# Output projection and first gate chunk of a two-layer trunk: the last three K pairs one token tile after the other, in an order by hand

## The chip, the cores and the metric

The kernel runs on one core of a Trainium2 chip. The core has five engines with an instruction queue each: TensorE (PE in the profile; its weight loads are listed as PEld), VectorE (DVE), ScalarE (ACT), GpSimd (POOL) and SyncE (SP), which here only issues DMAs. The metric is the device time of one execution in microseconds (us). Before the change the median of three runs is 2180.88 us (2180.05 to 2183.07).

## The reference

A trunk of two layers works on 256 tokens of width 2048, in fp32:

```
for l in range(DEPTH):                       # 2 layers
    h = rms_norm(x, pre_mix_norm[l])
    m = hybrid_mixer(h, ...)                 # h @ w_in, two kinds of attention, mix @ w_o
    x = x + rms_norm(m, post_mix_norm[l])
    h = rms_norm(x, pre_ffn_norm[l])
    f = (silu(h @ w_gate[l]) * (h @ w_up[l])) @ w_down[l]      # 2048 -> 5632 -> 2048
    x = x + rms_norm(f, post_ffn_norm[l])

rms_norm(x, g) = x * rsqrt(mean(x * x) + 1e-6) * g
```

The change lies where `mix @ w_o` ends, its norm is added to `x`, and the product of the new `x` with `w_gate` and `w_up` begins.

## The kernel before, in words

**Tiles.** The 256 tokens are two token tiles, t = 0 and 1, of 128. A product accumulates over K = 2048, that is 16 K tiles of 128, taken in eight *pairs* `kp`. Output columns are taken in chunks of 512: four for the output projection (c = 0 to 3), eleven for gate and up together.

**Split operands.** Every fp32 operand is split in a rounded part and a rest. For weights ACT writes `hi` (L307) and DVE `lo = raw - hi` (L317), 128x1024 elements each, that is a pair's two K tiles by 512 columns. A product of two such operands is three matmuls of 128x128 by 128x512 (hi hi, lo hi, hi lo). A *unit* (L560) of one token tile is a pair by 512 columns: six matmuls.

**Sevens.** For some pairs two chunks and two token tiles are taken together in seven products instead of eight (`seven_products`): they use sums of token blocks (`pair_sums`, L1237, then `token_sums`, L1091 to L1102: `s`, rounded to `sh` on ACT, its rest `sl` on DVE) and mixed weights (`mixed_weights`). For the latter a pair of weight tiles is loaded as `G` and `T`; POOL adds a half of G's data into `T` by an accumulating DMA (L258); ACT rounds `hi` and `Th`, DVE works out `lo`, differences in `T` (L290), sums in `G` (L291) and the rests `Tl` (L281).

**Loads.** Weights come in tiles of 512 KB, all in one stream order. SP issues plain tiles `raw` (L241, four buffers), `G` (L230) and `T` (L257). A load into a `raw` buffer waits for DVE to have taken the rest of the tile four before it. There are six buffers for `hi` and six for `lo`.

**Order.** Most instructions are ordered by a scheduler that lays out each engine's queue at build time. Within `tc.manual_schedule(engines=...)` the named engines take the order of the program text. `tc.issue_after(x)` keeps an instruction behind x in its queue; `weights(i, ahead)` emits the roundings of the stream's tiles up to `ahead` tiles beyond i.

**The stage.** The output projection's chunks 2 and 3 take pairs `LATE_O` = 4, 5, 0, 1, 6, 2 with both token tiles at once (5 and 6 as sevens; after pair 6 the parts that the sevens share are worked out by `shared_part` and added). Then `LAST_O` = 3, 7 go token tile by token tile, in an order by hand for ACT and DVE (L1185 on): four units of t = 0, the evacuation (`evac_sum`: multiply by the gain, ACT's square for the norm), `rescale` for t = 0 (the norm's root by Ln, Exp and a Newton step, then x = x + r * mg for four quarters of 512 columns, L627), then four units of t = 1, and after each of them one quarter of t = 0's new x is turned: four transposes on PE into one PSUM bank (L485), four roundings with the gain on ACT (L488), four rests on DVE (L493), giving the stationary tiles `xF`. After the block, t = 1 is evacuated, rescaled and turned quarter by quarter at high priority. `inv_rms` squares x again (L512, eight ACT instructions of 128x512) for the feed-forward norm's factor `rs`, which is only used at the end of a chunk.

**The gate's first chunk.** It takes the pairs in the order 0, 1, 3, 2, 7, 4, 6, 5 (`FIRST_ORDER`). Pairs 0 and 1 go token tile by token tile (t = 0 with both, then t = 1 with both), then 3, 2, 7 with both, 4 and 6 as sevens (L1084 to L1086), and 5 last. The plain pairs are `eight` (L1250): 24 matmuls for two token tiles. PE's order is the scheduler's throughout. `FORM_AT` says ahead of which pair of which chunk the sums of a seven's pair are emitted: here pair 4's ahead of the second of the remaining pairs (n = 1), pair 6's ahead of the third (n = 2).

Both layers run the same stage: about 376 to 442 us in layer 0, 1462 to 1528 us in layer 1.

## Time and profile before

| | |
|---|---|
| median of the runs | 2180.88 us (2180.05 to 2183.07) |
| profiled execution | 2183.48 us, of which 2181.7 us span |
| mean granted TensorE clock | 0.999 |
| PE busy | 2166.0 us (99%), 9944 matmuls |
| DVE busy | 1920.7 us (88%) |
| ACT busy | 1400.4 us (64%) |
| POOL busy | 260.5 us (12%) |
| L317 rests on DVE | 468 of 1220 ns |
| L307 roundings on ACT | 490 of 1053 ns |

A profile has one row for an instruction, or for several alike that follow each other: start in us from the span's start, length, engine, line, operation, output <- inputs, shape, count, and in brackets the idle time before it with what ended it. A matmul's length overlaps with the next one's: what it costs is the distance between starts. In a windows row stand the stretch, its length, then for each engine its busy time and the number of its instructions, PEclk (the granted clock, 1.00 is full), the DMA engines' busy share and GB/s. In a row of waits stand what waited, for what, the sum in us, the number and the longest.

### The profile page before, as it was taken

To read this page: it belongs to the slowest core of one execution; us is meant where nothing else is said; L and a number is where in the kernel's file an instruction comes from. 1 tells how busy PE (TensorE), PEld (TensorE's weight loads), DVE (VectorE), ACT (ScalarE), POOL (GpSimd) and SP (SyncE) were. 2 spreads that over 40 slices of the span, in tenths; PEclk is the share of its full clock that TensorE was granted. 3 is DMA by queue.
4 is the path that set the end of the run, shared out by engine and by line. 5 is a ranking of instruction groups with operands and counts; after the bars stand their busy time and mean duration, and the time that the engine had idled before them with its cause. 6 is when DMAs were issued, how large, how long until landed. Compare 5 with 4: busy or idle time off the path is not lost.

```text
span 2181.7 us, 28784 instructions
## 1 busy us (share of the span) xinstructions
PE 2166.0 (99%) x9944; PEld 1781.7 (82%) x9944; DVE 1920.7 (88%) x2657; ACT 1400.4 (64%) x2089; POOL 260.5 (12%) x243
## 2 busy tenths in 40 slices
PE   9999999999999999999999999999999999999998
PEld 7888888788888888888878888887888888888886
DVE  7888658899999999999878886589999999999997
ACT  7666665756666656666665666657666666576664
POOL 1100000031222221000010000000212222200000
PEclk9999999999999999999999999999999999999999
DMA  9544555488887767767465555555888877768683
GB/s 323 194 164 174 193 184 176 165 300 234 239 258 229 226 231 233 239 223 258 149 241 174 172 174 188 191 164 191 286 237 241 262 222 227 240 225 244 204 268 100
DMA packets 140851, 471.49 MB, mean 216 GB/s; under 512 B 16016, under 2 KB 17040, under 8 KB 140192
## 3 DMA queue, kind: packets, MB, share of 16 engines
q1 hardware_dynamic: 121952, 436.03, 57.7%
q0 software_dynamic: 18176, 33.07, 9.2%
q8 instruction: 78, 1.28, 0.2%
q14 instruction: 69, 0.57, 0.1%
q10 hardware_dynamic: 576, 0.54, 0.1%
HBM read 461.19 MB, written 8.39 MB: 215 GB/s over the span
## 4 chain that ended last, share of the span: by engine, by line
PE 94%; DVE 3%; ACT 2%; issue 1%; DMA 0%; SPq 0%; DVEq 0%; ACTq 0%
PE c L1250 19%; PE in L1084 7%; PE in L1086 7%; PE in L1085 7%; PE dn L1357 4%; PE dn L1356 4%; PE dn L1359 4%; PE p L1085 3%; PE c L1084 3%; PE p L1084 3%; PE p L1086 3%; PE c L1085 3%; PE c L1086 3%; PE o L569 2%; PE o L571 2%; PE o L570 2%
## 5 line engine op out<-in xcount | busy, mean ns | idle before, releaser
L317 DVE TENSOR_TENSOR lo<-raw,hi 128x1024 fp32r<-128x1024 f32 x468 | 561.9, 1220 | 103.3 <-ACT hi L307 102.3
L307 ACT ACTIVATE hi<-raw 128x1024 fp32r<-128x1024 f32 x490 | 501.5, 1053 | 102.3 <-DMA raw<-in_weights_in_turn_dram 41.8
L1250 PE MATMUL c<-hi,xF 128*128 128x512 f32 x1280 | 345.9, 391 | 1.5 <-DVE xF L493 1.5
L1250 PEld LDWEIGHTS c<-hi,xF 128*128 128x128 f32 x1280 | 238.3, 188 | 50.3 <-DVE xF L493 2.0
L258 POOL DMA_DIRECT2D T<-in_weights_in_turn_dram x126 | 111.2, 883 | 1373.8 <-DMA T<-in_weights_in_turn_dram 716.6
L1250 PE MATMUL c<-lo,xF 128*128 128x512 f32 x640 | 198.2, 390 | 2.5 <-DVE lo L317 2.5
L279 ACT ACTIVATE Th<-G 128x1024 fp32r<-128x1024 f32 x126 | 133.1, 1056 | 79.8 <-DVE G L291 78.6
L281 DVE TENSOR_TENSOR Tl<-G,Th 128x1024 fp32r<-128x1024 f32 x126 | 153.9, 1221 | 10.1 <-ACT Th L279 10.1
L1356 PE MATMUL dn<-hi,jh 128*128 128x512 f32 x416 | 162.0, 389 | 0.0
L1357 PE MATMUL dn<-lo,jh 128*128 128x512 f32 x416 | 161.8, 389 | 0.0
L307 ACT ACTIVATE hi<-G 128x1024 fp32r<-128x1024 f32 x126 | 132.9, 1055 | 44.6 <-DMA G<-in_weights_in_turn_dram 27.8
L281 DVE TENSOR_TENSOR lo<-T,hi 128x1024 fp32r<-128x1024 f32 x126 | 159.6, 1266 | 0.3 <-ACT hi L279 0.2
L279 ACT ACTIVATE Th<-T 128x512 fp32r<-128x512 f32 x126 | 79.7, 633 | 118.6 <-DVE T L290 113.3
L291 DVE TENSOR_TENSOR G<-G,T 128x1024 f32<-128x1024 f32 x126 | 153.5, 1218 | 1.8
L1250 PEld LDWEIGHTS c<-lo,xF 128*128 128x128 f32 x640 | 120.1, 188 | 28.1 <-DVE lo L317 3.0
L317 DVE TENSOR_TENSOR lo<-G,hi 128x1024 fp32r<-128x1024 f32 x108 | 131.6, 1219 | 12.3 <-ACT hi L307 12.2
L279 ACT ACTIVATE hi<-T 128x1024 fp32r<-128x1024 f32 x126 | 132.2, 1049 | 12.1 <-PE c L1086 10.6
L1084 PE MATMUL in<-hi,xT 128*128 128x512 f32 x328 | 131.0, 401 | 0.6 <-DVE xT L862 0.6
L1084 PE MATMUL in<-hi,xI 128*128 128x512 f32 x328 | 131.1, 401 | 0.0
L1085 PE MATMUL in<-lo,xI 128*128 128x512 f32 x328 | 128.0, 390 | 0.3 <-DVE lo L317 0.3
L1085 PE MATMUL in<-lo,xT 128*128 128x512 f32 x328 | 127.8, 391 | 0.4 <-DVE lo L891 0.4
L1359 PE MATMUL dn<-hi,jl 128*128 128x512 f32 x416 | 128.0, 389 | 0.0
(485 smaller groups left out, 4954.2 us busy)
## 6 DMA issues: line engine op xcount, KB each, us to landing
raw<-in_weights_in_turn_dram SPq DMA_DIRECT2D x490, 512.0 KB, 4.6
T<-in_weights_in_turn_dram SPq DMA_DIRECT2D x126, 512.0 KB, 5.3
G<-in_weights_in_turn_dram SPq DMA_DIRECT2D x126, 512.0 KB, 5.4
T<-in_weights_in_turn_dram POOLq DMA_DIRECT2D x126, 256.0 KB, 6.1
GU<-in_weights_in_turn_dram SPq DMA_DIRECT2D x32, 512.0 KB, 6.5
V<-in_weights_in_turn_dram SPq DMA_DIRECT2D x8, 512.0 KB, 3.7
away_ffn<-x SPq DMA_DIRECT2D x8, 512.0 KB, 8.2
xd<-away_ffn SPq DMA_DIRECT2D x8, 512.0 KB, 9.4
```

What stands on the lines that cost most here:

```text
L279: nc.scalar.activation(h, w, AF.Copy)
L281: newest_rest[i] = nc.vector.tensor_tensor(out=l, in0=w, in1=h.bitcast(F32), op=ALU.subtract)
L291: nc.vector.tensor_tensor(out=g, in0=g, in1=t2.unsqueeze(1).to_broadcast([P, 2, CW]), op=ALU.add)
L307: nc.scalar.activation(hi, raw, AF.Copy)
L317: rest = nc.vector.tensor_tensor(out=lo, in0=raw, in1=hi.bitcast(F32), op=ALU.subtract)
L1084: nc.tensor.matmul(a, sh, hi, start=first, stop=False, skip_group_check=open_sums[0])
L1085: nc.tensor.matmul(a, sh, lo, start=False, stop=False, skip_group_check=open_sums[0])
L1086: return nc.tensor.matmul(a, sl, hi, start=False, stop=last, skip_group_check=open_sums[0])
L1250: nc.tensor.matmul(a, stat[part], w[j][:, kk, :], start=first and kk + n == 0, stop=last and kk == 1 and n == 2)
L1356: nc.tensor.matmul(accs[c, t], sh, hi[:, kk, :], start=first, stop=False, skip_group_check=open_sums[0])
L1357: nc.tensor.matmul(accs[c, t], sh, lo[:, kk, :], start=False, stop=False, skip_group_check=open_sums[0])
L1359: nc.tensor.matmul(accs[c, t], sl, hi[:, kk, :], start=False, stop=last, skip_group_check=open_sums[0])
```

## The change

- Pair 2, the last of `LATE_O`, joins `LAST_O`: all six units of t = 0 (pairs 2, 3, 7 by chunks 2 and 3), then all six of t = 1. The shared parts of the sevens are worked out between t = 0's units.
- PE joins ACT and DVE in the order by hand, which now reaches into the gate's first chunk: pairs 0 and 1 (`first`, `second`) of t = 0, then of t = 1.
- `rescale` is taken apart (`root_of`, a generator in three steps, and `rescaled`, one quarter), and so is `transposed` (`turned_x`, `rounded_x`, `rest_of_x`). Inside the order by hand only quarters 0 and 1 of x are rescaled and turned: quarter 0 of t = 0 between t = 1's units, the others between the units of the gate. Quarters 3 and 2 follow behind `newest`, the last rest of quarter 1.
- `rounded_next` puts the next weight tile's rounding on ACT at one place and its rest on DVE at a later one.
- `inv_rms` is emitted ahead of the gate's fifth pair (n = 2), its squares behind `newest`.
- Both pair sums, 4 and 6, are emitted ahead of the fifth pair.
- In the stream's load order that results, four `raw` tiles go ahead of the first two `T` and `G`.

The numbers of matmuls, roundings, rests and loads are the same. The core of the diff:

```diff
-FORM_AT = {(0, 1): 4, (0, 2): 6, (0, 5): 5, (1, 3): 2, (2, 4): 3}
+FORM_AT = {(0, 2): (4, 6), (0, 5): (5,), (1, 3): (2,), (2, 4): (3,)}
...
+    def rounded_next():
+        i = fed[0]
+        fetch(i + 1)
+        raw = raws[i]
+        hi = wpool.tile([P, 2, CW], F32R, tag="hi", bufs=6, name=f"hi{i}")
+        nc.scalar.activation(hi, raw, AF.Copy)
+        lo = wpool.tile([P, 2, CW], F32R, tag="lo", bufs=6, name=f"lo{i}")
...
+        def rest(eng=nc.vector):
+            r = eng.tensor_tensor(out=lo, in0=raw, in1=hi.bitcast(F32), op=ALU.subtract)
...
-    def inv_rms(t, pool, nm, parts=None):
+    def inv_rms(t, pool, nm, parts=None, behind=None):
...
+                with tc.issue_after(behind.ins) if behind else nullcontext():
+                    nc.scalar.activation(junk, x_part(t, h * CW, CW), AF.Square, accum_out=part[:, h : h + 1])
...
-        for kp in LATE_O:
+        for kp in LATE_O[:-1]:
...
-        last_o = [(c, kp) for c in (2, 3) for kp in LAST_O]
-        with tc.manual_schedule(engines={mybir.EngineType.Activation, mybir.EngineType.DVE}):
-            feed(idx + 6)
-            for n, (c, kp) in enumerate(last_o):
-                unit({0: accs[c, 0]}, mix, idx + n, kp, (0,), False, kp == LAST_O[-1], 0)
-                if kp == LAST_O[-1]:
-                    evac_sum(pool, accs[c, 0], mg, ssm, gpost, c, 0, f"o{l}")
-            rescale(mg, ssm, 0, f"o{l}")
-            for n, (c, kp) in enumerate(last_o):
...
-                unit({1: accs[c, 1]}, mix, idx + n, kp, (1,), False, kp == LAST_O[-1], 0)
-                transposed(0, 32 + l * KT, xT, cols=(n,))
...
-        with tc.high_priority(offset=URGENT):
-            evac_sum(pool, accs[3, 1], mg, ssm, gpost, 3, 1, f"o{l}", True)
-            rescale(mg, ssm, 1, f"o{l}", lambda t, c: transposed(t, 32 + l * KT, xT, cols=(c,)))
...
+        late = [(c, LATE_O[-1]) for c in (2, 3)] + [(c, kp) for c in (2, 3) for kp in LAST_O]
...
+        by_hand = {mybir.EngineType.Activation, mybir.EngineType.DVE, mybir.EngineType.PE}
+        with tc.manual_schedule(engines=by_hand):
+            last_units(0, (0, 1))
+            nc.scalar.copy(m[0], p1)
+            nc.vector.tensor_tensor(out=m[1], in0=p6, in1=m[0], op=ALU.subtract)
+            nc.vector.tensor_tensor(out=m[2], in0=p7, in1=m[1], op=ALU.add)
+            feed(idx + 4)
...
+            last_units(0, (2, 3))
+            squared(pool, shared_added(accs[2, 0], mg, 2, 0), ssm, 2, 0, nm)
+            gain(2, 0)
+            last_units(0, (4, 5))
+            last_units(1, (0, 1))
+            squared(pool, shared_added(accs[3, 0], mg, 3, 0), ssm, 3, 0, nm)
+            root = root_of(ssm, 0, nm)
...
+            rests_next = [rounded_next()]
+            gain(3, 0)
+            r = [next(root)]
+            rescaled(mg, 0, 0, r[0])
+            last_units(1, (2,))
+            pb = [turned_x(0, 0)]
+            last_units(1, (3, 4, 5))
...
+            fetch(fed[0] + 4)
...
+            eight(first_banks, 0, first, (0,), True, False, ahead=0)
+            eight(first_banks, 0, second, (0,), False, False, (0,), 0)
+            squared(pool, accs[3, 1], ssm, 3, 1, nm)
+            root = root_of(ssm, 1, nm)
...
+            gain(2, 1)
+            r.append(next(root))
+            rescaled(mg, 1, 0, r[1])
+            pb.append(turned_x(1, 0))
+            eight(first_banks, 0, second, (0,), False, False, (1,), 0)
+            gain(3, 1)
+            columns(pb[1], 1, 0)
+            rescaled(mg, 0, 1, r[0])
+            eight(first_banks, 0, first, (1,), True, False, ahead=0)
+            pb.append(turned_x(0, 1))
+            rounded_x(pb[2], 0, 1, g0, xT)
+            rescaled(mg, 1, 1, r[1])
+            rests_next.pop(0)()
+            rests_next.append(rounded_next())
+            rest_of_x(pb[2], 0, 1, g0, xT)
+            eight(first_banks, 0, second, (1,), False, False, (0,), 0)
+            pb.append(turned_x(1, 1))
+            rounded_x(pb[3], 1, 1, g0, xT)
+            rests_next.pop(0)()
+            eight(first_banks, 0, second, (1,), False, False, (1,), 0)
+            newest = rest_of_x(pb[3], 1, 1, g0, xT)
+        eight(first_banks, 0, third, range(NT), False, False)
+        for cg in (3, 2):
+            for t in range(NT):
+                with tc.issue_after(newest.ins):
+                    rescaled(mg, t, cg, r[t])
+                columns(turned_x(t, cg), t, cg)
+        eight(first_banks, 0, fourth, range(NT), False, False, ahead=2)
...
-        rs = [inv_rms(t, pool, f"ffn{l}") for t in range(NT)]
...
+                if (c, n) == (0, 2):
+                    rs = [inv_rms(t, pool, f"ffn{l}", behind=newest) for t in range(NT)]
```

## The prediction

> **What bounds the kernel now.** I read the page's busy shares, then TensorE's waits, then windows around the changed stage, then that stage row by row.

> ```profile
> span 2181.7 us, 28784 instructions
> PE 2166.0 (99%) x9944; PEld 1781.7 (82%) x9944; DVE 1920.7 (88%) x2657; ACT 1400.4 (64%) x2089; POOL 260.5 (12%) x243
> ```
> ```profile
> PE c L1250 <- DVE lo L317: 2.5, 2, 1.3
> ...
> PE c L1250 <- DVE xF L493: 1.5, 2, 0.7
> ```
> ```profile
> core 0: us, PE busy (x) PEld busy (x) DVE busy (x) ACT busy (x) POOL busy (x), PEclk, DMA share, GB/s
> 376.60:427.20 50.60, 48.52 (x225) 39.22 (x225) 44.40 (x100) 34.65 (x83) 1.76 (x2) 1.00 0.57 192
> 376.60:436.10 59.50, 57.42 (x264) 46.25 (x264) 53.30 (x111) 41.05 (x90) 1.76 (x2) 1.00 0.51 173
> 1462.60:1513.20 50.60, 48.52 (x226) 39.27 (x225) 44.47 (x100) 34.69 (x83) 1.77 (x2) 1.00 0.57 191
> ```
> TensorE is busy 99% of the span, so only its stalls can be won. Two of its largest, 1.3 and 0.7 us, fall once in each layer at the hand-over from output projection to gate (L1250). Both layers run this stage alike (50.60 us, 48.52 busy), so I work out layer 0 and double it. VectorE is the second bound: over 376.6 to 436.1 it works 53.30 of 59.50 us and has 6.2 us to spare.

> **What can be won.** TensorE in this stage (start, length; in brackets the wait):

> ```profile
> 376.64 0.39 PE L569 MATMUL o<-hi,mix_sb 128*128 128x512 f32 x1
> ...
> 396.42 0.96 PE L1250 MATMUL c<-hi,xF 128*128 128x512 f32 x3 [0.74 <-DVE xF L493]
> ...
> 406.21 0.50 PE L1250 MATMUL c<-lo,xF 128*128 128x512 f32 x1 [1.25 <-DVE lo L317]
> ...
> 409.75 0.60 PE L485 MATMUL xT_ps<-ident,x 128*128 128x128 f32 x4
> 410.10 0.95 PE L1250 MATMUL c<-hi,xF 128*128 128x512 f32 x3
> 410.88 0.62 PE L1250 MATMUL c<-lo,xF 128*128 128x512 f32 x2
> ...
> 427.26 0.39 PE L1084 MATMUL p<-hi,xF 128*128 128x512 f32 x1
> ...
> 437.44 0.39 PE L1085 MATMUL p<-Tl,sh 128*128 128x512 f32 x1
> ...
> 442.43 0.39 PE L1250 MATMUL c<-hi,xF 128*128 128x512 f32 x1
> ```
> From 437.44 to 442.43 are 22 matmuls without a stall: 0.2268 each. Four transposes and three matmuls take 410.88-409.75 = 1.13, so a group of four costs 0.45. Pair 2's first matmul (376.64) to the first seven (427.26) is 50.62 us for 192 matmuls (43.55) and 8 groups (3.60): 47.15 of work and 3.5 lost. That 3.5 per layer, 7 in all, is the ceiling of a gain here.

> **The change, step by step.** Matmuls, roundings, rests and loads stay the same in number; only their order moves.

> ```profile
> 388.70 0.68 DVE L589 TENSOR_TENSOR mg_o<-o,mg_o 128x512 f32<-128x512 f32 x1
> ...
> 392.23 0.75 DVE L627 SCALAR_TENSOR_TENSOR x<-mg_o,tot_o,x 128x512 f32<-128x512 f32 x1
> ```
> ```profile
> 406.07 2.15 DVE L493 SCALAR_TENSOR_TENSOR xF<-xT_ps,gains,xF 128x128 fp32r<-128x128 f32 x8
> ...
> 426.24 0.42 DVE L1237 TENSOR_TENSOR f<-xF 128x256 f32<-128x256 f32 x1
> 426.58 0.28 DVE L1093 TENSOR_TENSOR s<-f 128x128 f32<-128x128 f32 x1
> 426.78 0.28 DVE L1091 TENSOR_TENSOR s<-f 128x128 f32<-128x128 f32 x1
> ...
> 434.27 0.68 DVE L281 TENSOR_TENSOR Tl<-T,Th 128x512 fp32r<-128x512 f32 x1
> 434.87 1.22 DVE L317 TENSOR_TENSOR lo<-raw,hi 128x1024 fp32r<-128x1024 f32 x1
> 436.01 1.22 DVE L281 TENSOR_TENSOR Tl<-G,Th 128x1024 fp32r<-128x1024 f32 x1
> ```
> ```profile
> 393.04 1.32 PE L485 MATMUL xT_ps<-ident,x 128*128 128x128 f32 x8
> ```
> ```profile
> 393.73 1.14 ACT L488 ACTIVATE xF<-xT_ps,gains 128x128 fp32r<-128x128 f32 x4 [1.03 <-PE xT_ps L485]
> ...
> 402.00 0.76 ACT L512 ACTIVATE junk_ffn<-x 128x512 f32<-128x512 f32 x1
> ...
> 402.62 0.75 ACT L512 ACTIVATE junk_ffn<-x 128x512 f32<-128x512 f32 x1
> ...
> 416.81 1.05 ACT L307 ACTIVATE hi<-G 128x1024 fp32r<-128x1024 f32 x1
> ```
> Starts in these rows give what one step holds its engine: a rest of the weights 1.14 (434.87 to 436.01), a half one 0.60, a rest of x 0.26, a pair sum's two kinds 0.34 and 0.20, a square 0.62.

> *The shared part.* Its copy and six VectorE steps, 0.60 each, now stand between token 0's units. Units of 12 matmuls (2.7 us) hide them, and VectorE's evacuation waits for the second pair of units anyway; if a rounding came late here, a unit would start late by as much, at most the 0.7 to which the rows of before put such waits.

> *Token 0 first.* Its 36 matmuls now end at 376.64+36x0.2268 = 384.8, not after pair 2 of both tokens. In the rows above, last evacuation to first rescaled quarter took 392.98-388.70 = 4.28; one gain now stands behind the root, so about 3.4: quarter 0 is ready at 388.3 to 389.2. TensorE wants it after 54 matmuls, at 388.9: no stall, at most 0.3. The gate starts after 72 matmuls and one group, 376.64+16.33+0.45 = 393.4, instead of 396.42: the 0.7 wait is gone.

> *Token 1's quarter 0.* Its transposes stand behind 18 gate matmuls, at 397.5. From transposes to the last of four roundings took 393.04 to 394.87, 1.83, so VectorE's rests start at 399.4, while its hand order has nothing for it after the two gains (about 397.3): 2.0 idle, and TensorE waits 0.5 at the gate's token 1 (399.8). *Quarter 1* again: transposes at 399.8+12x0.2268 = 402.5, rests at 404.4, VectorE out of work at 402.9: 1.5 idle. These waits queue everything behind them on VectorE.

> *Quarters 3 and 2.* From 404.4 VectorE has 24 rests of x (6.2), five of weights (5.7) and four rescaled quarters (4 x 0.66 = 2.6), 0.4 of small waits: 419.4. TensorE's own work hides all of it but 0.1, as third and fourth pair lie between.

> *Squares behind the newest rest.* Before they filled gaps from 402.0; now eight, 5.0 us, run on ACT from 418.2 to 423.4 in one row. VectorE waits 1.35 for the first four (420.75) and 1.15 for an Exp that stands behind the sixth. The first mixed weights' rounding waits behind them: 423.4 instead of 416.81.

> *Both pair sums at one place, loads turned round.* No work added. SP's and POOL's order:

> ```profile
> 406.60 0.90 SPq L257 DMA_DIRECT2D T<-in_weights_in_turn_dram  x2
> 407.54 0.93 SPq L230 DMA_DIRECT2D G<-in_weights_in_turn_dram  x2
> 411.81 7.25 SPq L241 DMA_DIRECT2D raw<-in_weights_in_turn_dram  x4
> ```
> ```profile
> 411.57 0.89 POOL L258 DMA_DIRECT2D T<-in_weights_in_turn_dram  x1 [261.72 <-DMA T<-in_weights_in_turn_dram]
> ```
> ```profile
> raw<-in_weights_in_turn_dram SPq DMA_DIRECT2D x5, 512.0 KB, 4.8
> T<-in_weights_in_turn_dram SPq DMA_DIRECT2D x2, 512.0 KB, 4.8
> ...
> T<-in_weights_in_turn_dram POOLq DMA_DIRECT2D x2, 256.0 KB, 6.8
> ```
> (The last fence is the stretch 405 to 420: size and median time from issue to landing.)
> T and G went ahead of four raw tiles; now they stand behind them, and each raw tile waits on SP for a rest on VectorE, the last at 412.5. So the first T issues at 413.0 (406.60 before), lands 4.8 later, and POOL's add into it, another 6.8, is done at 424.6: just when ACT comes to it behind the squares and one rounding (423.4+1.06 = 424.5). As computed the turn costs nothing, but nothing covers it any more; its bounds are 0 and, with a landing one us slower, 1.15 a layer.

> **The sum.** TensorE reaches the first seven at 376.64+47.15+0.5 = 424.3, 3.0 earlier. VectorE leaves the squares' chain at 422.6 and then must do, before the last rest that chunk 0 needs: nine steps of 1.14 (six weight rests, the two additions into G, one Tl from G: 10.3), six of 0.60 (two differences in T, two Tl from T, two sl: 3.6), four pair additions (1.4), eight 128-wide ones (1.6) and 0.4 of small ones, 17.3 without a gap: 439.9. That last one is the rest of pair 5's up weight; before it is the row at 434.87, ending at 436.09. Added this way the rows of before come out 0.2 short, so 440.1, four us later. In the changed instruction order 16 matmuls stand from the one that waits for it to the place that was at 442.43; the others that before still had there (22 from 437.44) have been moved ahead as fillers: 440.1+0.2+16x0.2268 = 443.9, against 442.43. So 3.0 are won and about 4.5 given back in the two sevens: +1.5 per layer. A first matmul behind a wait holds its place 0.1 longer than others, and there will be about ten short waits, of which only those behind the last one count fully: I take +1.8, +3.6 in all. The bounds are +1.4 (no restart counts) and +2.9 (C below) a layer. No later stage has TensorE waits that could take it up. The profiled execution took 2183.48, so it would become 2187.1; the median of the three runs is 2.6 lower, and on that I forecast 2184.5. A gain or loss of 0.2%, 4.4 us, is about what a measurement of this kernel can tell from no change.

> [...] Across the 1.25 us wait at 406.21 the windows show PEclk 1.00: the granted clock did not fall. [...]

> **Rivals.**
> B, the other side: the sevens do not wait. The scheduler has fillers (pair 5, chunk 1's first matmuls), and VectorE had 6.2 us to spare. It decides if the last rest comes by 438.5, 1.6 earlier than I have it; if it comes by 437, all of the 3.0 stays: 2174.9. Against it: the waits above add up to 6.0 us of idle on VectorE between 397 and 422.3 alone, and nothing idles behind that, so it cannot catch up.
> C, T late: one landing a us later than I took (6.8 is itself the slow end; the four bunched raw tiles take their share of the queues) moves ACT's T rounding and all behind it: +1.15 per layer; the same if pair 7's second raw tile, whose load waits on SP for a rest at 406.6, lands a us later than I took and holds the rest at 411.3 with the four rescaled quarters behind it. 2 x 2.9 = 5.8: 2186.7, to 2189 with both.
> D, the clock falls in the chain of waits: 21 matmuls at twice 0.2268 cost 4.8 per layer: 2194. For it: ten waits in 16 us. Against: PEclk 1.00 above.
> E, both cancel: the change does nothing that shows, 2180 to 2182.

> **How the numbers follow.** Forecast 0.52 (own range 2182.5 to 2187; over the bound at 2185.2 about 0.15 of it), C 0.26 (nearly all over), B 0.13 (0.11 under 2176.5), E 0.06, D 0.03. Faster 0.11, same 0.37+0.01+0.02+0.06 = 0.46, slower 0.43. The range 2177 to 2189 leaves out the better part of B and D, some 0.13, and a little of C.

> **What would show it.** Right: the gate's first matmul some 16.8 us behind pair 2's first, no 1.25 wait, the first seven 47.5 to 48.5 behind, then waits of TensorE for L1127 and L1128 operands from DVE and ACT, 4 to 5 us per layer; eight squares in a row on ACT; chunk 1 1.5 to 2 us later than before, counted from pair 2. Wrong: sevens without waits, or stalls at the quarters' transposes, where my slack is only 0.3.

## The result, and the profile after

The changed kernel takes 2186.94 us (median of 10 runs, 2184.17 to 2188.32) against 2180.85 us of the kernel before (10 runs, 2180.05 to 2183.07): a ratio of 1.0025 with a 95% interval of 1.0016 to 1.0035, some 6 us slower. The page of its profiled execution (2184.17 us, the shortest of the ten):

```profile
span 2182.5 us, 28761 instructions
...
PE 2165.1 (99%) x9944; PEld 1781.2 (82%) x9944; DVE 1920.9 (88%) x2657; ACT 1403.0 (64%) x2089; POOL 252.3 (12%) x243
```

The shares are those of before; only the stage tells the change. TensorE's waits over the whole execution after it:

```profile
PE q L1127 <- ACT sh L1144: 2.6, 2, 1.5
...
PE p L1128 <- DVE Tl L281: 1.2, 2, 0.7
...
PE p L1127 <- ACT Th L279: 0.6, 2, 0.3
PE q L1128 <- DVE lo L281: 0.5, 1, 0.5
PE c L1245 <- DVE xF L516: 0.5, 2, 0.2
```

The waits of 1.3 and 0.7 us at L1250 are gone. In their place stand waits inside the sevens (L1127 and L1128) for rounded sums, rests and mixed weights. TensorE's rows in layer 0, first of the kernel before (a second profile of it, taken in the study) and then of the changed one:

```profile
375.93 0.39 PE L569 MATMUL o<-hi,mix_sb 128*128 128x512 f32 x1
...
426.53 0.39 PE L1084 MATMUL p<-hi,xF 128*128 128x512 f32 x1
...
489.10 0.61 PE L1250 MATMUL c<-lo,xF 128*128 128x512 f32 x2
```

```profile
375.76 0.39 PE L599 MATMUL o<-hi,mix_sb 128*128 128x512 f32 x1
...
392.58 0.62 PE L1245 MATMUL c<-hi,xF 128*128 128x512 f32 x2
...
398.88 0.73 PE L1245 MATMUL c<-hi,xF 128*128 128x512 f32 x2 [0.23 <-DVE xF L516]
...
423.56 0.44 PE L1127 MATMUL p<-hi,xF 128*128 128x512 f32 x1
...
425.35 0.50 PE L1127 MATMUL q<-hi,sh 128*128 128x512 f32 x1 [1.12 <-ACT sh L1144]
...
473.77 0.50 PE L1128 MATMUL p<-Tl,sh 128*128 128x512 f32 x1 [0.73 <-DVE Tl L281]
...
491.12 0.62 PE L1245 MATMUL c<-lo,xF 128*128 128x512 f32 x2
```

From pair 2's first matmul to the first seven it was 50.60 us and is 47.80: 2.8 won. To the same two matmuls of chunk 2 (the last row of each fence, after equally many TensorE instructions) it was 113.17 and is 115.36: 2.2 lost, so 5.0 were given back in between. Layer 1 loses 2.3. Of these 4.5 us in all, about 1.6 come back later: chunks 2 to 10 of this execution have fewer small waits than those of the kernel before.

VectorE and ACT of the changed kernel show what TensorE waited for:

```profile
398.47 1.12 DVE L516 SCALAR_TENSOR_TENSOR xF<-xT_ps,gains,xF 128x128 fp32r<-128x128 f32 x4 [2.02 <-ACT xF L508]
...
403.56 1.12 DVE L516 SCALAR_TENSOR_TENSOR xF<-xT_ps,gains,xF 128x128 fp32r<-128x128 f32 x4 [1.50 <-ACT xF L508]
...
419.82 0.16 DVE L545 TENSOR_REDUCE ssx_ffn<-ssp_ffn 128x1 f32<-128x4 f32 x1 [1.31 <-ACT junk_ffn L542]
...
421.31 0.22 DVE L495 SCALAR_TENSOR_TENSOR rsq_ffn<-rs_ffn,rsq_ffn 128x1 f32<-128x1 f32 x1 [1.15 <-ACT rs_ffn L484]
...
437.64 1.22 DVE L317 TENSOR_TENSOR lo<-raw,hi 128x1024 fp32r<-128x1024 f32 x1
```

```profile
417.11 0.75 ACT L542 ACTIVATE junk_ffn<-x 128x512 f32<-128x512 f32 x1
...
422.30 1.14 ACT L307 ACTIVATE hi<-G 128x1024 fp32r<-128x1024 f32 x1
```

VectorE stands idle four times, 6.0 us together, and has nothing to idle on afterwards: the rest of pair 5's up weight ends 63.1 us behind pair 2's first matmul, 3.7 later than before. ACT comes to the first mixed weight only when the squares are done.

### The profile page after: what moved, and what is told of

It reads as the page before. It is cut to its first block, busy times and chain, and to the rows that moved or that the text cites. A ratio compares the mean times of both kernels' runs of the same rounds, so it can differ in the third digit from the quotient of the medians.

```text
span 2182.5 us, 28761 instructions
## 1 busy us (share of the span) xinstructions
PE 2165.1 (99%) x9944; PEld 1781.2 (82%) x9944; DVE 1920.9 (88%) x2657; ACT 1403.0 (64%) x2089; POOL 252.3 (12%) x243
## 3 DMA queue, kind: packets, MB, share of 16 engines
q8 instruction: 78, 1.28, 0.2%
## 4 chain that ended last, share of the span: by engine, by line
PE 92%; DVE 4%; ACT 2%; issue 1%; DMA 1%; DVEq 0%; SPq 0%; ACTq 0%
PE c L1245 18%; PE in L1127 7%; PE in L1129 7%; PE in L1128 7%; PE dn L1466 4%; PE dn L1465 4%; PE dn L1468 4%; PE p L1128 3%; PE p L1129 3%; PE c L1129 3%; PE c L1128 3%; PE c L1127 3%; PE p L1127 3%; PE o L599 2%; PE o L601 2%; PE o L600 2%
## 5 line engine op out<-in xcount | busy, mean ns | idle before, releaser
L317 DVE TENSOR_TENSOR lo<-raw,hi 128x1024 fp32r<-128x1024 f32 x456 | 546.2, 1220 | 99.2 <-ACT hi L307 98.1
L307 ACT ACTIVATE hi<-raw 128x1024 fp32r<-128x1024 f32 x478 | 488.5, 1053 | 96.0 <-DMA raw<-in_weights_in_turn_dram 46.0
L258 POOL DMA_DIRECT2D T<-in_weights_in_turn_dram x126 | 111.3, 883 | 1376.9 <-DMA T<-in_weights_in_turn_dram 380.1
L281 DVE TENSOR_TENSOR Tl<-G,Th 128x1024 fp32r<-128x1024 f32 x126 | 153.9, 1222 | 10.1 <-ACT Th L279 10.1
L307 ACT ACTIVATE hi<-G 128x1024 fp32r<-128x1024 f32 x126 | 133.3, 1058 | 43.5 <-DMA G<-in_weights_in_turn_dram 27.0
L281 DVE TENSOR_TENSOR lo<-T,hi 128x1024 fp32r<-128x1024 f32 x126 | 158.3, 1256 | 0.2 <-ACT hi L279 0.2
L317 DVE TENSOR_TENSOR lo<-G,hi 128x1024 fp32r<-128x1024 f32 x108 | 131.6, 1219 | 7.9 <-ACT hi L307 7.8
L1127 PE MATMUL in<-hi,xT 128*128 128x512 f32 x328 | 131.0, 401 | 0.7 <-ACT hi L932 0.7
L1127 PE MATMUL in<-hi,xI 128*128 128x512 f32 x328 | 131.2, 401 | 0.0
L1128 PE MATMUL in<-lo,xI 128*128 128x512 f32 x328 | 128.0, 390 | 0.3 <-DVE lo L317 0.3
L1129 PE MATMUL in<-hi,xI 128*128 128x512 f32 x328 | 128.0, 391 | 0.0
## 6 DMA issues: line engine op xcount, KB each, us to landing
raw<-in_weights_in_turn_dram SPq DMA_DIRECT2D x490, 512.0 KB, 4.6
T<-in_weights_in_turn_dram SPq DMA_DIRECT2D x126, 512.0 KB, 5.4
G<-in_weights_in_turn_dram SPq DMA_DIRECT2D x126, 512.0 KB, 5.1
T<-in_weights_in_turn_dram POOLq DMA_DIRECT2D x126, 256.0 KB, 6.0
GU<-in_weights_in_turn_dram SPq DMA_DIRECT2D x32, 512.0 KB, 6.3
V<-in_weights_in_turn_dram SPq DMA_DIRECT2D x8, 512.0 KB, 3.7
away_ffn<-x SPq DMA_DIRECT2D x8, 512.0 KB, 7.9
xd<-away_ffn SPq DMA_DIRECT2D x8, 512.0 KB, 9.6
```

Source lines behind the costliest of these rows:

```text
L281: newest_rest[i] = nc.vector.tensor_tensor(out=l, in0=w, in1=h.bitcast(F32), op=ALU.subtract)
L307: nc.scalar.activation(hi, raw, AF.Copy)
L317: rest = nc.vector.tensor_tensor(out=lo, in0=raw, in1=hi.bitcast(F32), op=ALU.subtract)
L1127: nc.tensor.matmul(a, sh, hi, start=first, stop=False, skip_group_check=open_sums[0])
L1128: nc.tensor.matmul(a, sh, lo, start=False, stop=False, skip_group_check=open_sums[0])
L1129: return nc.tensor.matmul(a, sl, hi, start=False, stop=last, skip_group_check=open_sums[0])
```

## The experiments

All but before_again, which is a single execution, were timed in several rounds beside the kernel before. Beside the ratio stands the length from pair 2's first matmul to the 504th TensorE instruction behind it, which is the second matmul of the rows at 489.10 and 491.12 above; it needs no other part of the execution. It is 113.39 and 113.43 us (layers 0 and 1) in the kernel before and 115.59 and 115.69 in the first profile of the changed one. This stretch is called *the stretch* below. The edit of loads_turned leaves TensorE's order as it is; in the other edited kernels the scheduler also puts some TensorE instructions of the stage at other places (from 48 of the 9944 in rests_filled to 156 in all_three; squares_late, below, moves more), so these runs show an edit together with that.

**The two kernels once more.** No edit.

> The changed kernel once more, for a second profile of it and as the measure for the runs beside it. Theory (VectorE comes late to the two sevens, by waits in its hand order and by the squares): again some 2.2 us per layer lost between pair 2's first matmul and the end of the gate's first chunk, 6 us over the kernel before. Rival (the clock or the chip, not the stage): the stage's loss differs from the first profile's by more than 0.5 us.

Measured: 2187.36 us, ratio 1.0028 (1.0017 to 1.0039). The stretch is 116.29 and 116.27 us, 2.9 longer than before, not 2.2. That differs from the first profile by 0.6 to 0.7 us, more than the 0.5 set for the rival, so the loss itself varies. The rows of layer 1 in this execution (TensorE, then ACT, then the granted clock in slices of 2 us) show two things that vary:

```profile
1513.44 0.50 PE L1127 MATMUL q<-hi,sh 128*128 128x512 f32 x1 [2.03 <-ACT sh L1144]
1513.78 0.53 PE L1127 MATMUL c<-hi,sh 128*128 128x512 f32 x1
1514.10 0.63 PE L1128 MATMUL p<-lo,xF 128*128 128x512 f32 x1
1514.53 0.63 PE L1129 MATMUL p<-hi,xF 128*128 128x512 f32 x1
```

```profile
1511.72 1.06 ACT L279 ACTIVATE hi<-T 128x1024 fp32r<-128x1024 f32 x1 [0.91 <-DMA T<-in_weights_in_turn_dram]
```

```profile
1512.00:1514.00 2.00, 0.56 (x2) 0.97 0.08 16
1514.00:1516.00 2.00, 2.00 (x6) 0.50 0.00 0
1516.00:1518.00 2.00, 2.00 (x8) 0.68 0.00 0
```

Here T came 0.91 us after ACT was ready for it. ACT's rounding of the sums stands behind T's, so TensorE waited 2.03 us instead of the 1.50 of this layer in the first profile. After that stall the granted clock was 0.50 for some 3 us, with matmuls 0.43 us apart. In layer 0 the clock kept its full rate and T came 0.37 us late; in the first profile T was late by 0 and 0.38 us (layers 0 and 1).

> The kernel before once more, for a second profile of it. Theory (the loss lies in the stage; the later chunks' small waits in the first profile of the kernel before are that execution's own): the stage from pair 2's first matmul to chunk 1 agrees with the first profile within 0.3 us in both layers, and the waits between 590 and 850 us are smaller. Rival (the later waits belong to the kernel before and hide a part of any loss): the same waits again, about 2 us in layer 0.

Measured: 2181.51 us, one run. The stage agrees with the first profile of before within 0.02 us at the stretch's end in both layers. The later chunks, from chunk 2 to the end of the gate, took 0.8 and 0.5 us less than in the first profile: that part of the later waits was that execution's own.

**The squares later, in the wrong place.**

```diff
-                if (c, n) == (0, 2):
+                if (c, n) == (0, 5):
                     rs = [inv_rms(t, pool, f"ffn{l}", behind=newest) for t in range(NT)]
```

> The changed kernel with the feed-forward norm's eight squares emitted ahead of the gate's last pair instead of the fifth. Theory: ACT comes to the mixed weights about 5 us earlier, VectorE loses its 1.3 and 1.15 us waits; TensorE's 1.5 and 0.9 us waits in the first seven go; 1.8 to 2.6 us per layer gained on the changed kernel, 3.6 to 5 in all. Rival (T comes late by its load order): T's add lands at about 424 as before, ACT waits for it instead and less than 0.5 us per layer is gained.

Measured: 2233.73 us, ratio 1.0237 (1.0220 to 1.0255). To the first seven and through chunk 0 it was 1.5 to 2.4 us per layer better than the changed kernel, as the theory has it, but by the end of the gate each layer was 26 to 31 us behind the kernel before. This run does not tell the theories apart: the scheduler laid out chunks 1 to 9 in another order (572 TensorE instructions at other places), and on ACT the end of the norm's root now stood between two Silus, with three table loads of 1.28 us each at 453 to 459 us instead of one. The trace also shows 21 VectorE steps, against 6 in the changed kernel, that lasted until just after a POOL rest of a weight tile, 39 us in all beyond the usual length of their kind (6 us there); so a stretched step can have had a large part in the loss, which no run separates. TensorE's largest wait over the execution:

```profile
PE p L1127 <- DVE w L1412: 23.9, 13, 3.6
```

**Two rests into VectorE's idle time.** The rests of the next two weight tiles move ahead of the rests of x that VectorE waited for.

```diff
-            columns(pb[1], 1, 0)
+            rounded_x(pb[1], 1, 0, g0, xT)
+            rests_next.pop(0)()
+            rest_of_x(pb[1], 1, 0, g0, xT)
+            rests_next.append(rounded_next())
             rescaled(mg, 0, 1, r[0])
...
             rests_next.pop(0)()
-            rests_next.append(rounded_next())
             rest_of_x(pb[2], 0, 1, g0, xT)
...
             rounded_x(pb[3], 1, 1, g0, xT)
-            rests_next.pop(0)()
```

> The changed kernel with two weight rests moved by hand into VectorE's 2.0 and 1.5 us of idle time ahead of the rests of quarters 0 (token 1) and 1 (token 0). Theory: everything behind them on VectorE comes 1.6 us earlier per layer, the sevens wait less by as much: 3.2 us in all. Rival (T late, or only the squares count): VectorE's idle time moves to the place before the sevens, under 0.5 us per layer.

Measured: 2183.92 us, ratio 1.0011 (1.0002 to 1.0020), 3.4 us less than the changed kernel beside it; the stretch is 114.64 and 114.23 us. The theory's 3.2 us came by the medians; by the stretch it is 2.4 us over both layers against the first profile and 3.7 against the second. In layer 0 VectorE's waits of 2.0 and 1.5 us are down to 0.9 and 0.3, that before the rests of quarters 3 and 2 grew from 0.2 to 1.2, and what stands behind came 1.3 us earlier instead of 1.6. The order by hand on VectorE cost a little more than half of the loss.

**T and G ahead of the raw tiles.**

```diff
-            with not_ahead(i) if mixing else nullcontext():
+            with not_ahead(i) if mixing else tc.issue_after(newest_sum[0].ins) if i in behind_sums else nullcontext():
                 loads.append(nc.sync.dma_start(raw, stream[i]))
```

Here `behind_sums` holds pair 5's gate tile of each layer, and `newest_sum` the last load into T.

> The changed kernel with pair 5's raw loads held behind the first two T loads, so that T and G go ahead of four raw tiles as in the kernel before. Theory: T lands some 5 us earlier but ACT is at its squares, so nothing is gained: within 0.3 us per layer of the changed kernel. Rival (T late): 1 us or more per layer gained.

Measured: 2186.28 us, ratio 1.0022 (1.0013 to 1.0031), 1.1 us less than the changed kernel beside it. POOL's add into T in layer 0 began at 412.84 us, 35.5 us behind pair 2's first matmul (377.35 here); in the changed kernel it is 43.2 us behind it (418.96). POOL's row, and TensorE's wait between 376 and 480 us:

```profile
412.84 0.89 POOL L261 DMA_DIRECT2D T<-in_weights_in_turn_dram  x1 [262.29 <-PE c L1248]
```

```profile
PE q L1130 <- ACT sh L1147: 1.0, 1, 1.0
```

TensorE's wait for the rounded sums is 1.0 us here in layer 0, where the two profiles of the changed kernel, both layers, have 1.1 to 2.0. ACT never waits for T here, so the 1.0 us is left without a late T, and T's load adds what it is late by in a given execution, up to 0.9. Between the theory (0.3 per layer) and the rival (1 or more) the medians come out at 0.5, nearer the theory; but the intervals of the two ratios overlap, and the stretch, 116.11 and 115.63 us, lies between 115.6 and 116.3 as in the two profiles of the changed kernel, so a gain of 1.1 us is not shown.

**The squares one seven later, then with the rests, then with the loads as well.** The first is the edit of squares_late with `(0, 4)`, the second adds that of rests_filled, the third that of loads_turned.

> The changed kernel with the squares emitted ahead of the gate's seventh pair (pair 6) instead of the fifth; this time no engine's order differs behind the stage. Theory: TensorE's 1.5 and 0.9 us waits in the first seven go, the second seven still waits for VectorE's Tl: 2.0 to 2.4 us per layer gained on the changed kernel, so 4 to 5 us in all, near the kernel before. Rival (T late): under 0.5 us per layer.

> The squares as in squares_n4 and the two weight rests as in rests_filled. Theory: 0.8 us per layer more than squares_n4 alone, as now T, whose load stands behind four raw tiles, sets the end of the first seven. Rival (no third limit): the two gains add up, 1.3 us per layer more.

> Squares, weight rests and the T loads ahead of pair 5's raw tiles. Theory: with all three the sevens wait for nothing and the 2.7 us per layer that the hand-over wins stay: 5 us under the kernel before, 0.25%. Rival (another limit takes over, such as the loads of pair 5 or G): 2 us or less under it.

Measured: 2184.91 us, ratio 1.0011 (1.0002 to 1.0020); 2186.38 us, ratio 1.0016 (1.0007 to 1.0025); 2182.72 us, ratio 1.0002 (0.9993 to 1.0011). The stretch is 114.33 and 114.71 us in the first, 114.95 and 115.74 in the second, 114.40 and 114.41 in the third. The first wins about 3 us on the changed kernel instead of 4 to 5; the second gets no better, and worse by its medians and by the stretch; and the third is level with the kernel before instead of 5 us under it: its rival was right. All three lost it at one place. At chunk 1 there is a gap between matmul starts of 1.16 to 1.18 us in the first, 2.16 and 2.19 in the second and 2.16 and 2.20 in the third (layers 0 and 1). In the sevens the second also waits 1.4 us (layer 0) and 0.6 (layer 1) for a mixed weight from ACT, which had itself waited 1.8 and 1.4 us for T, as its theory has it. In the third no wait is left in the first chunk's sevens, so its rows show the new one best (TensorE, VectorE, POOL, and the clock):

```profile
439.49 0.61 PE L1248 MATMUL c<-hi,xF 128*128 128x512 f32 x2
441.88 0.73 PE L1248 MATMUL c<-hi,xF 128*128 128x512 f32 x2 [1.77 <-DVE w L1172]
```

```profile
438.69 2.46 DVE L498 SCALAR_TENSOR_TENSOR rsq_ffn<-rs_ffn,rsq_ffn 128x1 f32<-128x1 f32 x2
441.08 0.15 DVE L499 SCALAR_TENSOR_TENSOR rs_ffn<-rsq_ffn,rs_ffn 128x1 f32<-128x1 f32 x1
441.15 0.68 DVE L1172 TENSOR_TENSOR w<-p,w 128x512 f32<-128x512 f32 x1
```

```profile
437.76 3.25 POOL L313 TENSOR_TENSOR lo<-raw,hi 128x1024 fp32r<-128x1024 f32 x1 [27.58 <-ACT rs_ffn L487]
```

```profile
440.00:442.00 2.00, 0.23 (x2) 1.00 0.22 88
442.00:444.00 2.00, 2.00 (x7) 0.68 0.99 213
444.00:446.00 2.00, 2.00 (x6) 0.50 1.07 306
446.00:448.00 2.00, 2.00 (x10) 0.96 1.05 374
```

A Newton step of one column (0.22 us at 421.31 above) lasted until POOL's rest of a weight tile ended at 441.01. Behind it stood the step that empties the bank in which chunk 1 begins to accumulate. The squares moved later had brought the norm's Newton steps into the time of POOL's rest. There the first of the two took about 2.3 us and the second 0.2, and the first ended 0.02 us behind POOL's rest; what held it no row shows. After the stall of 2.2 us the clock fell to half for some 3.4 us, in both layers of this run.

**The squares earlier instead.** Four of the eight go by hand into ACT's idle time between the roundings of x, the other four stay.

```diff
             columns(pb[1], 1, 0)
+            for u in range(NT):
+                square_of_x(u, 0, pool, f"ffn{l}", ssp[u])
             rescaled(mg, 0, 1, r[0])
+            square_of_x(0, 1, pool, f"ffn{l}", ssp[0])
...
             rounded_x(pb[3], 1, 1, g0, xT)
+            square_of_x(1, 1, pool, f"ffn{l}", ssp[1])
...
-                    rs = [inv_rms(t, pool, f"ffn{l}", behind=newest) for t in range(NT)]
+                    rs = [inv_rms(t, pool, f"ffn{l}", behind=newest, part=ssp[t]) for t in range(NT)]
```

`square_of_x` is one square of a quarter, and `inv_rms` with `part` does quarters 2 and 3 alone. The second kernel has the edits of rests_filled and loads_turned as well, with token 0's second square one place later, behind the rounding of its quarter 1; in the third the other four squares are emitted at `(0, 3)`.

> The changed kernel with four of the eight squares (quarters 0 and 1 of both token tiles) put by hand into ACT's idle time between the roundings of x; the other four stay where they were. Theory (the squares ahead of the mixed weights cost): ACT comes to them 2.5 us earlier, TensorE's 1.5 us wait in the first seven goes, 1.5 to 1.8 us per layer gained on the changed kernel; and as the norm's Newton steps stay at about 421, they meet no tensor operation of POOL. Rival (ACT's place does not matter, T does): less than 0.5 us per layer.

> squares_early with the weight rests of rests_filled and the load order of loads_turned. Theory: what is left of waits in the sevens is about 0.6 us, none of TensorE's stalls is longer than 0.7 us, so the clock keeps its full rate; 1.9 us per layer under the kernel before, 2177 to 2179. Rival (VectorE has too much work in the stage whatever its order): the lost time turns up at chunk 1 as in all_three, level with the kernel before.

> The same with the last four squares emitted one pair later, behind the first mixed weights' roundings. Theory: 0.8 us per layer better still, since the sevens wait for nothing; the Newton steps come at 432 to 437, ahead of POOL's rest for chunk 1 at about 438. Rival (Newton steps meet POOL's rest and VectorE stands still, as in all_three): a wait of 1 to 2 us at chunk 1 and level with the kernel before or worse.

Measured: 2183.77 us, ratio 1.0015 (1.0006 to 1.0024); 2179.24 us, ratio 0.9993 (0.9984 to 1.0002); 2177.33 us (11 runs, 2175.11 to 2178.71), ratio 0.9983 (0.9974 to 0.9991). The stretch is 114.85 and 114.75 us in the first, 1.4 to 1.5 less than in the profile of the changed kernel taken with after_again, near the 1.5 to 1.8 expected, but 0.7 and 0.9 less than in the first; 112.75 and 112.49 in the second, 0.6 and 0.9 under the kernel before where 1.9 was expected; 110.95 and 111.73 in the third, 2.4 and 1.7 under it. In the first ACT was ready for the mixed weights 1.6 us earlier than in the changed kernel, counted from pair 2 (2.5 expected), but then waited 0.9 and 1.3 us for G and 1.1 and 0.8 for T (layers 0 and 1): with the squares out of the way the loads are the next limit. What the second lacks stands at chunk 1, where TensorE waits 0.8 us for Tl in the second seven of both layers. The third beats both kernels, by a gain that is small (0.17%) but clear of the noise; in layer 1 it still waits 0.8 us for Tl in chunk 1, and in layer 0 its only wait of TensorE between 376 and 480 us, its Newton steps, and POOL's rest behind them:

```profile
PE c L1254 <- DVE xF L519: 0.2, 1, 0.2
```

```profile
434.69 0.34 DVE L498 SCALAR_TENSOR_TENSOR rsq_ffn<-rs_ffn,rsq_ffn 128x1 f32<-128x1 f32 x2
434.95 0.15 DVE L499 SCALAR_TENSOR_TENSOR rs_ffn<-rsq_ffn,rs_ffn 128x1 f32<-128x1 f32 x1
```

```profile
438.28 2.58 POOL L313 TENSOR_TENSOR lo<-raw,hi 128x1024 fp32r<-128x1024 f32 x1 [27.55 <-ACT hi L310]
```

Two Newton steps take 0.34 us there. Of the hand-over's gain, which the prediction put at 3.0 per layer and which measured 2.8, the 2.4 and 1.7 us are thus kept to the stretch's end, as VectorE and ACT are kept busy in its shade.

## Why the prediction was right or wrong

It forecast 2184.5 us and 2177 to 2189; measured are 2186.94 and 2187.36. The direction and the mechanism were right, and the size was short by 2 to 2.5 us (3.6 over the kernel before forecast, 5.6 and 6.1 measured).

- *The hand-over.* Forecast: gate's first matmul 16.8 us behind pair 2's first, the first seven 47.5 to 48.5. Measured 16.82 and 47.80. Token 0's quarter came in time, token 1's cost 0.23 us of wait (0.5 forecast).
- *VectorE's idle time.* Forecast 2.0, 1.5, 1.35 and 1.15 us; measured 2.02, 1.50, 1.31 and 1.15. That these waits queue everything behind them was tested: with two rests moved into them 3.4 us came back.
- *The squares.* Forecast: ACT reaches the mixed weights at 423.4 us instead of 416.81. Measured 422.30, which is 423.2 in the times of the prediction's profile, where pair 2's first matmul stood 0.88 us later; with half of the squares put elsewhere (squares_early) the time above the kernel before was 2.7 to 3.1 us less by the medians and 2.2 to 2.8 by the ratios.
- *The last rest of chunk 0.* Forecast 440.1, which is 63.5 us behind pair 2's first matmul; measured 63.1.
- *The sum stopped too early.* This is the step that failed: "No later stage has TensorE waits that could take it up", and with it the assumption that nothing is added behind chunk 0. Up to chunk 1's first matmuls the sum held: at the place of the prediction's row at 442.43 (the 290th TensorE instruction behind pair 2's first) the loss against the kernel before was 1.1 and 1.6 us (layers 0 and 1) in the first profile and 1.5 and 2.1 in the second, with 1.8 forecast. But VectorE stayed late into chunk 1, whose second seven waits for Tl (the 0.73 at 473.77), with a gap between matmul starts of 1.13 us in layer 0 of the first profile and up to 1.17 in the second; there 0.7 to 1.4 us more were lost per layer. On the other side the later chunks took 1.6 us up again in the first profile and 1.1 in the second, as in the kernel before some matmuls of their sevens start 0.1 to 0.2 us late and in the changed one they do not; what they wait for is too short to stand in the rows. Forecast per layer 1.8; the stretch measured 2.2 to 2.9.
- *Rival C, T late.* It had been given 0.26 and proved to be a part, not an alternative: T was late by 0 to 0.9 us depending on the execution, and with its load put first the median was 1.1 us lower, which the intervals do not separate from nothing. That T came so near the forecast was in part luck: its load took 7.0 us to land instead of 4.8, and POOL's add 5.0 instead of 6.8 (medians of 405 to 425 in the first profile), and the two errors cancel.
- *Rival D, the clock.* It had been given 0.03 and does happen, in one layer of one of the two profiles of the changed kernel, behind a stall longer than the forecast had: a gap of 2.42 us between matmul starts was enough. The 21 matmuls at twice 0.2268 and the 4.8 us per layer of this rival no run of the stage shows: in all_three 7 or 8 matmuls went 0.43 us apart, and in layer 1 of squares_n4_filled the fall cost 1.6 us.
- *Rival B, the other side.* It was to decide at a last rest by 438.5. It came at 438.9, which is 439.7 in the prediction's times, and the changed kernel was slower; early_filled_turned_n3 is what B looks like when the rests do come in time.
- *What stays open.* The medians are 5.6 to 6.1 us apart, the spans of the two profiles of the changed kernel 2.7 and 4.6 us above the second profile of the kernel before (2179.8), on both sides of the 3.6 forecast; so what is missing lies mostly in executions that left no rows. Those other executions are 0.4 to 4.2 us longer than these two. A varying T and spells at half clock could do a part of that; it was not shown. The clock alone does not do it: of the seven executions in after_again the shortest has the spell at half clock (mean granted clock 0.998), and the longest, 2190.22 us, has 0.999.

## What to carry to other kernels

When an engine near its limit (VectorE, 53 of 59 us) paces what comes after a stall, removing the stall on TensorE gains only what that engine can also be brought forward; add up its idle time in the new order, place by place, before counting a gain, and follow the lateness past the first place where it shows. In an order by hand a wait holds up what is queued behind it (in layer 0 of rests_filled, with two rests moved into VectorE's waits of 2.0 and 1.5 us, what stood behind came 1.3 us earlier), so the next independent step belongs into each gap, and work that is needed late should go into gaps that are there early rather than be pushed back to where it meets something else. What a late step meets there (another engine's long instruction, a bank to be emptied) can cost more than the step: in all_three a step of 0.2 us lasted 2.3, and TensorE's gap behind it was 2.2 us.

## What the runs showed of the hardware

```profile
439.33:442.74 3.41, 1.64 (x8) 1.00 0.56 167
442.74:446.15 3.41, 3.41 (x10) 0.50 1.02 282
...
442.08:445.50 3.42, 1.65 (x8) 1.00 0.40 128
445.50:448.91 3.41, 3.41 (x17) 1.00 1.01 291
...
2173.52:2176.94 3.42, 1.71 (x4) 1.00 0.00 0
2176.94:2180.35 3.41, 0.18 (x1) 1.00 0.94 303
...
1736.43:1739.85 3.42, 1.85 (x9) 1.00 0.46 158
1739.85:1743.26 3.41, 1.38 (x6) 1.00 0.78 280
1743.26:1746.67 3.41, 3.41 (x10) 0.50 0.56 197
```

Of these stretches at full clock, those with 0.18, 1.38 and 1.64 us of work were followed by half clock (that of 0.18 by 0.50 from 2180.35 to the kernel's end), those with 1.65, 1.71 and 1.85 were not. In these rows half clock did not follow by the length of a gap alone. Gaps between matmul starts of 2.16 and 2.20 us (all_three), 2.19 (squares_n4_filled, layer 1) and 2.42 (after_again, layer 1) lay in one stretch and were followed by half clock; one of 2.16 (squares_n4_filled, layer 0, from 441.76) lay across the boundary at 442.08 and was not, nor was one of 2.31 near the end of the changed kernel (from 2173.70), whose stretch had 1.71 us of work. Twenty TensorE instructions across the gap took 6.6 us in layer 0 of squares_n4_filled and 8.2 in layer 1, so the fall cost 1.6 us there.
- *In all_three a VectorE step of one column lasted 2.3 us* instead of 0.2, from 438.69 until POOL's rest of a weight tile (437.76 to 441.01) had ended, while a 128x512 step that reads a PSUM bank and one SBUF tile kept its 0.68 us beside such a rest (at 447.18 in the changed kernel, where POOL's ran from 446.41 to 449.52). This is no peculiarity of the moved steps: in all thirteen profiles every VectorE step that lasted over 0.3 us beyond the usual of its shape (6 to 21 in a profile) ended 0.02 to 1.1 us behind a POOL rest of a weight tile. In the changed kernel a 128x128 pair addition at 448.97 us took 0.70 instead of 0.28 and ended 0.15 behind POOL's rest.
